# Layer 0's dense products: plain float32 matmuls on unsplit operands in the place of three float32r matmuls on split ones

## The chip, the cores and the metric

The kernel runs on one core of a Trainium2 chip. The metric is device time in microseconds, the median of several executions; lower is better. The engines are TensorE (PE in the profile; PEld is its weight load), VectorE (DVE), ScalarE (ACT), GpSimd (POOL) and SyncE (SP), which issues the DMAs.

## The reference, cut to what matters

A trunk of two layers over 512 tokens of 1024 channels. Only layer 0's mixers and their output projection matter here:

```python
z = rmsnorm(h, mix_norm[j]) @ mix_w_in[j]
y_a = rwkv7_bidir(z[..., :RWKV_COLS], ...)      # 8 heads x 64, one scan per direction
y_b = hyena_bidir(z[..., RWKV_COLS:], ...)      # 512 channels, long filters through an FFT
h = h + jnp.concatenate([y_a, y_b], axis=-1) @ mix_w_out[j]
...
h = h + conv_ffn(h, ...)
h = h + per_layer_embedding(h, p[i], ...)       # sigmoid(rmsnorm(h) @ w_gate) * (p_i @ w_proj)
```

Layer 1 has neighbourhood attention in the mixers' place, then the same two blocks.

## The kernel before

Channels lie on the partitions, 128 at a time, and the 512 tokens along the free dimension. Everything is float32 in DRAM.

**Split products.** A large product is made of three float32r matmuls: each operand is split into a high part, rounded to float32r, and a low part, the rest (`split`, lines 361 to 368; `mm3`, 370 to 373). ScalarE writes the high part, VectorE or GpSimd the low one. The feed-forward blocks, layer 1 and the late output projection (`gemm`, `load_split`) do this too, with their own loops and buffers.

**Layer 0's mixers** (`both_mixers`, from line 703) are one stage with two kinds of work:

- a *main line* of dense products, unit after unit in a fixed order: the input projection (26 tiles of 128 columns, eight products each; `columns`, 859), the projections of the per-layer embeddings (`embedding`, 1384), Hyena's transforms (`forward`, 1403) as products with tables of cosines and sines, the early part of the output projection (`out_early`, 1476: row tiles 0 to 2), and the transform back (`inverse`, 1448);
- *chains* of small steps beside it: the norm (`norm0`, 827), the preparation of each head pair and direction (`rwkv_prep`), the inverses of triangular matrices (`inverse_ab`), the scans over chunks of 64 tokens (`scan`), the group norm and gate (`rwkv_out`), the filters and the products of spectra (`filter_parts`, `spectrum`).

`drive` (670) writes the two out in one order. It keeps a plan (`Pace`, 205 to 313) of when each engine will have done what is written so far; when a chain's next stage is planned to be ready, the stage is written, else the next product of the main line. Where the planned TensorE work of the last 3.4 us falls under 5000 columns, the main line goes first. `in_order` (558) then holds every engine to that written order, so a step that is late on the chip holds up what is written behind it on its engine. The plan's price of a matmul is columns x passes / 2400 us, with 1 pass for float32r, 2 for a transpose and 4 for float32 (lines 272 to 277); that of a VectorE instruction is 0.07 + 0.00106 us a column (282).

**Operands of the main line.** Weights and tables come as slabs of 128x512 float32 (`stream`, 588): up to three are loaded ahead, and up to three more are split ahead (`feed`, 619, when the plan says that the load has landed; `parts`, 581: ScalarE copies to float32r at line 584, GpSimd subtracts). A slab of weights serves four products. The tables of the transforms are stored already split in DRAM and are only cast, the high part by ScalarE (611), the low one by GpSimd (612). The layer's input, the signals, the filters' sums and the spectra are split where they are made. There are 59 slabs.

**After the mixers** `outproj0` (1551) adds the late row tiles of the output projection with `gemm`; its operands come from `out_parts` (1352), which waits until the input projection no longer reads the buffers that they go to.

Of the kernel before, what the change touches and what calls it, by code (L numbers as in the profile page):

```python
# [32 lines left out]
# ---------------------------------------------------------------- layout of the weights  # L33
# [14 lines left out]
# row tiles of layer 0's output projection: those of its early part, and the others  # L48
# [20 lines left out]
def _kc(n):  # L69
    """Row tiles of weights in a chunk of n column tiles."""  # L70
    return (8, 4, 2, 2)[n - 1]
# [13 lines left out]
# columns of the packed per-channel parameters: name -> number of columns  # L85
# [32 lines left out]
# ---------------------------------------------------------------- constants of the shapes  # L118
# [14 lines left out]


def _hi(a):
    a = np.ascontiguousarray(a, dtype=np.float32)
    b = a.view(np.uint32)
    r = ((b >> 12) & 1) + np.uint32(0x7FF)
    return ((b + r) & np.uint32(0xFFFFF000)).view(np.float32)


def _constants():
# [18 lines left out]
    # transforms at the frequencies (2f+1)pi/1024, f < 256; even and odd times apart, which gives those of 511 - f  # L161
# [6 lines left out]
    inv = parts.transpose(0, 2, 1).reshape(4, 2, P, S)  # part, fc, f, time  # L168
    c["dft_i"] = np.ascontiguousarray(inv.transpose(1, 2, 0, 3)).reshape(2, P, 2048)
    # filter features and decay window  # L170
# [10 lines left out]
def _rpb_table(rpb):  # L181
    """Relative position bias as each (16-column query block, head) reads it, both by columns of the grid;
    -1e30 outside the window."""
# [16 lines left out]
    t = np.stack(out, axis=2).reshape(8, 2, P, 3, 256)  # pair, head, q, table, key  # L200
# [3 lines left out]
# ---------------------------------------------------------------- the kernel  # L204
class Pace:
    """Estimates of when what is written so far will have run. The order in which the rest is written follows them;
    nothing that is computed depends on them."""
# [15 lines left out]
    @staticmethod  # L223
    def area(x):
        """Name, first and last row, first and last column."""
        size = math.prod(x.tensor.shape[1:])
        p, f = divmod(x.offset, size)
        p1, f1 = p, f
        for i, (step, n) in enumerate(x.ap):
            if i == 0 and step == size:  # L230
                p1 += n - 1
            elif step < 0:
                f += step * (n - 1)
            else:
                f1 += step * (n - 1)
        return x.tensor.name, (p, p1, f, f1)
# [23 lines left out]
    # TensorE runs at half its clock after a stretch of this many us in which it streamed less than so many columns  # L260
# [5 lines left out]
    def density(self, t):  # L266
        """Columns streamed in the last TICK us before t."""
# [48 lines left out]
class Kern:  # L316
# [5 lines left out]
    # -- helpers  # L322
# [38 lines left out]
    def split(self, h, l, src, scale=None):  # L361
        """h + l = src (* scale), each in float32r."""
# [12 lines left out]
    def load_split(self, src, width, dt=F32):  # L375
        """One chunk of weights: from DRAM and into its two parts."""
# [7 lines left out]
    def gemm(self, wname, g, k0, k1, xs, evac, then=None):  # L384
        """then: what goes in between after two chunks of weights."""
# [77 lines left out]
    def conv3(self, out, u, w, b):  # L463
        """Centred depthwise convolution of width 3 over the tokens."""
# [9 lines left out]
    # -- the whole  # L474
# [42 lines left out]
    def mixer0(self):  # L517
# [5 lines left out]
        # tiles in DRAM  # L523
# [34 lines left out]
    def in_order(self, start):  # L558
        """Keeps the compute engines to the order in which everything from instruction start on is written."""
# [11 lines left out]
    # -- small helpers: slabs of SBUF, a bank of PSUM  # L571
# [9 lines left out]
    def parts(self, src):  # L581
        """A slab's two parts; the second one by GpSimd."""
        h, l = self.slab(F32R), self.slab(F32R)
        self.nc.scalar.copy(h, src)  # L584
        self.tt(l, src, h.bitcast(F32), ALU.subtract, self.nc.gpsimd)
        return h, l

    def stream(self, items):
        """Slabs from DRAM in their two parts, loaded and split ahead of their use. An item with two sources has its
        parts in them."""  # L590
        self.loads, self.split_ = deque(), deque()
        todo = iter(items)

        def load():
            srcs = next(todo, None)
            if srcs is not None:
                t = [self.slab() for _ in srcs]
                for x, y in zip(t, srcs):
                    self.nc.sync.dma_start(out=x, in_=y)
                self.loads.append(t)  # L600

        for _ in range(self.LOADS):
            load()
        yield
        while True:
            t = self.loads.popleft()
            if len(t) == 1:
                r = self.parts(t[0])
            else:
                r = [self.slab(F32R) for _ in t]  # L610
                self.nc.scalar.copy(r[0], t[0])
                self.nc.gpsimd.tensor_copy(out=r[1], in_=t[1])
            self.split_.append(r)
            load()
            yield
# [12 lines left out]
    def weights(self, name, g):  # L628
        """The slabs of a group of columns."""
# [5 lines left out]
        for k in range(0, K // P, KC):  # L635
            nk = min(KC, K // P - k)
            src = self.a[name][base + k * P * W:base + (k + nk) * P * W].rearrange("(p a) -> p a", p=P)
            out += [(src[:, i:i + 512],) for i in range(0, nk * W, 512)]
        return out

    def table(self, name, fc, j):
        src = self.a[name][fc]
        return src[:, j * 1024:j * 1024 + 512], src[:, j * 1024 + 512:j * 1024 + 1024]
# [8 lines left out]
    def put(self, out, in_):  # L652
        """A store, written once its data should be there, so that its queue doesn't wait."""
# [16 lines left out]
    def drive(self):  # L670
        """Stages of the chains as they can go, and the main line between them."""
        nc, pace, over, row = self.nc, self.pace, False, 0
        while self.chains or not over:
            now = pace.now()
            self.flush(now)
            self.feed(now)
# [26 lines left out]
    def both_mixers(self):  # L703
# [26 lines left out]
        def embed():  # L730
            if emb:
                l, g, j = emb.pop(0)
                what = [(a["pT"][l, k],) for k in range(2)] if (g, j) == (0, 0) else []
# [43 lines left out]
        # loads in the order of their use  # L777
# [3 lines left out]
        self.ws = self.stream(items)  # L781
        for k in range(KT):
            nc.sync.dma_start(out=xin[k], in_=a["xT"][k])
            if k == 0:
                next(self.ws)
# [6 lines left out]
        n = PAR_OFF["na_norm"]  # L792
        nc.sync.dma_start(out=self.prm[:, n:], in_=a["params"][:, n:])
# [8 lines left out]
        # 1 - mu; k_a / 2 and 1 - k_a / 2; w0 / 2, a0 / 2  # L802
# [56 lines left out]
    def columns(self, out):  # L859
        """A tile of columns of the input projection."""  # L860
        ps = self.bank()
        for half in range(2):
            hi, lo = self.item()
            for kk in range(4):
                k = half * 4 + kk
                c = slice(kk * P, (kk + 1) * P)
                while len(self.xs) <= k:
                    yield 0
                self.mm3(ps, hi[:, c], lo[:, c], *self.xs[k], k == 0, k == KT - 1)
                if k < KT - 1:  # L870
                    yield 0.65
# [5 lines left out]
        yield 0.65  # L877
# [45 lines left out]
    def rsqrt8(self, sq, scale, eps, op1=ALU.add):  # L923
        """The powers -1/2 of the sums over 64 channels, with the tokens on the partitions."""
# [10 lines left out]
    def spread(self, r):  # L935
        """... over 128 columns a tile of tokens ..."""
# [5 lines left out]
    def back(self, ex):  # L942
        """... and back with the channels on the partitions."""
# [7 lines left out]
    def rwkv_prep(self, m, d, zz):  # L951
        """Of one direction, in the order of its scan and chunk by chunk: k and r with the running decay, the update
# [894 lines left out]
```

## Time and profile before

| | us |
|---|---|
| time, median of 3 runs | 1636.56 |
| lowest and highest of them | 1633.0, 1638.45 |
| the profiled execution, its span | 1633.0 |
| TensorE busy in the span | 1541.6 (94%) |
| VectorE busy in the span | 1047.9 (64%) |
| ScalarE busy in the span | 681.0 (42%) |
| GpSimd busy in the span | 341.3 (21%) |

The span of the profiled execution and the lowest of the times are the same number: nothing of the time that is measured lies around the span.

The profile lists instructions by line, engine, operation and tiles: `b<-xh,w` is a matmul into a PSUM bank `b` from the input's high part `xh` and a slab `w`; `g` are the banks of the later blocks. Nearly every matmul has line 350, that of a helper, and all slabs are called `w`, so groups are told apart by tiles and shapes. "x464" counts instructions; behind the bar stand busy time and the mean ns of one, then the idle time of the engine ahead of them and what ended it. Matmuls overlap, so the mean is from start to end of one, not the distance to the next. The profile names both kinds of matmul f32 and shows float32r on what is written by the other engines alone (fp32r).

### The profile page before, as it was taken

The numbers are of one execution on the slowest core, as the hardware profiler recorded it, in microseconds if no ns is written. First come the engines' busy times: TensorE is split into PE (matmuls) and PEld (weight loads), VectorE is DVE, ScalarE is ACT, GpSimd is POOL, SyncE is SP. The second block draws the span as 40 slices with busy tenths as digits, with TensorE's granted clock in tenths as the row PEclk, the third lists the DMA queues.
The fourth block names the chain that finished last, engine by engine and source line by source line (L and its number), as shares of the span: only waits on it lengthen the run. The fifth ranks groups of instructions, "written<-read, shape, count | busy, mean of one in ns | idle before, by whom it ended". The sixth has DMA issues, their size and how long they took to land.

```text
span 1633.0 us, 24094 instructions
## 1 busy us (share of the span) xinstructions
PE 1541.6 (94%) x9296; PEld 1216.2 (74%) x9296; DVE 1047.9 (64%) x1740; ACT 681.0 (42%) x1082; POOL 341.3 (21%) x286
## 2 busy tenths in 40 slices
PE   7998798979898999999999989999999999999997
PEld 4675576766667888888888778777777888888886
DVE  7579868876876677534684664565666665276654
ACT  6464224333514544313443553565554442144432
POOL 3585525533721200000001322011030000000020
PEclk9999899899999999999999999999999999999999
DMA  6455638465764232222322433323112332322341
GB/s 202 136 141 137 188 105 237 136 215 157 232 214 167 100 103 90 96 99 90 103 91 96 137 116 103 106 83 123 66 65 78 103 104 90 98 88 93 110 142 65
DMA packets 116308, 200.13 MB, mean 123 GB/s; under 512 B 27729, under 2 KB 57297, under 8 KB 116194
## 3 DMA queue, kind: packets, MB, share of 16 engines
q1 hardware_dynamic: 116194, 198.59, 37.9%
q8 instruction: 73, 1.20, 0.3%
q14 instruction: 41, 0.34, 0.1%
HBM read 166.04 MB, written 30.93 MB: 121 GB/s over the span
## 4 chain that ended last, share of the span: by engine, by line
PE 76%; DVE 11%; issue 5%; ACT 3%; DMA 2%; POOL 2%; SPq 2%; POOLq 0%; DVEq 0%; ACTq 0%
PE g L350 60%; PE b L350 11%; DVE w L356 4%; DVE w L353 3%; PE m L350 1%; PE s L350 1%; PE m L1792 1%; ACT w L359 1%; POOL w L356 1%; DVE w L1168 1%; POOL rr L356 0%; ACT oh L364 0%; DVE ol L356 0%; DMA ch_d<-w 0%; POOL nacc L356 0%
## 5 line engine op out<-in xcount | busy, mean ns | idle before, releaser
L356 DVE TENSOR_TENSOR wlo<-wraw,whi 128x1024 fp32r<-128x1024 f32 x186 | 235.6, 1268 | 334.7 <-ACT whi L364 334.5
L364 ACT CAST whi<-wraw 128x1024 fp32r<-128x1024 f32 x186 | 194.2, 1044 | 426.8 <-PE g L350 410.2
L350 PE MATMUL g<-xh,whi 128*128 128x512 f32 x872 | 341.5, 392 | 5.4 <-ACT whi L364 5.4
L350 PE MATMUL g<-xl,whi 128*128 128x512 f32 x872 | 340.5, 390 | 0.0
L350 PE MATMUL g<-xh,wlo 128*128 128x512 f32 x872 | 340.3, 390 | 0.0
L356 POOL TENSOR_TENSOR w<-w 128x512 fp32r<-128x512 f32 (+2 forms) x142 | 184.0, 1317 | 166.7 <-ACT w L584 95.8
L350 PEld LDWEIGHTS g<-xh,whi 128*128 128x128 f32 x872 | 164.2, 188 | 41.2 <-ACT whi L364 5.6
L350 PEld LDWEIGHTS g<-xh,wlo 128*128 128x128 f32 x872 | 164.1, 188 | 34.9 <-DVE wlo L356 0.8
L350 PEld LDWEIGHTS g<-xl,whi 128*128 128x128 f32 x872 | 164.3, 188 | 33.7
L350 PE MATMUL b<-xh,w 128*128 128x512 f32 x464 | 172.4, 427 | 7.4 <-ACT xh L359 7.3
L356 POOL TENSOR_TENSOR nacc<-nsq 128x512 f32<-128x512 f32 x5 | 9.3, 1865 | 779.8 <-ACT nsq L359 779.8
L350 PE MATMUL b<-w 64*64 64x64 f32 (+6 forms) x1884 | 131.2, 271 | 17.5 <-DVE w L353 7.5
L350 PE MATMUL g<-hh,wlo 128*128 128x512 f32 x352 | 139.0, 395 | 0.0
L350 PE MATMUL g<-hl,whi 128*128 128x512 f32 x352 | 139.0, 395 | 0.0
L350 PE MATMUL g<-hh,whi 128*128 128x512 f32 x352 | 138.9, 395 | 0.0
L353 DVE SCALAR_TENSOR_TENSOR c<-u,prm,c 128x511 f32<-128x511 f32 x176 | 126.6, 748 | 6.9 <-ACT c L359 6.3
L350 PEld LDWEIGHTS b<-w 64*64 64x64 f32 (+4 forms) x1884 | 94.6, 142 | 44.1 <-POOL w L356 10.4
L350 PEld LDWEIGHTS b<-xh,w 128*128 128x128 f32 x464 | 91.6, 197 | 36.8 <-ACT xh L359 8.0
L359 ACT ACTIVATE c<-u,prm 128x512 f32<-128x512 f32 x88 | 70.0, 817 | 71.4 <-DVE u L356 71.4
L350 PE MATMUL b<-xl,w 128*128 128x512 f32 x232 | 95.7, 413 | 1.6 <-DVE xl L353 1.4
L356 DVE TENSOR_TENSOR w<-w 128x512 f32<-128x512 f32 (+16 forms) x127 | 88.8, 708 | 3.8 <-DMA w<-hw_d 1.0
L356 DVE TENSOR_TENSOR u<-g,rstd 128x512 f32<-128x512 f32 x104 | 71.5, 687 | 14.2 <-PE g L350 13.4
(178 smaller groups left out, 2344.0 us busy)
## 6 DMA issues: line engine op xcount, KB each, us to landing
wraw<-in_up SPq DMA_DIRECT2D x88, 512.0 KB, 3.5
wraw<-in_down SPq DMA_DIRECT2D x44, 512.0 KB, 3.4
w<-in_mix_w_in SPq DMA_DIRECT2D x52, 256.0 KB, 3.8
wraw<-in_na_w_qkv SPq DMA_DIRECT2D x24, 512.0 KB, 3.5
x<-ch_d SPq DMA_DIRECT2D x16, 640.0 KB, 5.9
ch_d<-w SPq DMA_DIRECT2D x64, 128.0 KB, 2.7
wraw<-in_gate SPq DMA_DIRECT2D x16, 512.0 KB, 3.5
tab<-in_rpb SPq DMA_DIRECT2D x8, 768.0 KB, 4.3
```

What stands on the lines that cost most here:

```text
L350: return self.nc.tensor.matmul(out, lhsT, rhs, start=start, stop=stop)
L353: return self.nc.vector.scalar_tensor_tensor(out=out, in0=in0, scalar=scalar, in1=in1, op0=op0, op1=op1)
L356: return (eng or self.nc.vector).tensor_tensor(out=out, in0=in0, in1=in1, op=op)
L359: return self.nc.scalar.activation(out=out, in_=in_, func=func, **kw)
L364: self.nc.scalar.copy(h, src)
L1168: nc.vector.tensor_reduce(out=x[:, i, 0:i], in_=tv, axis=AX.X, op=ALU.add)
L1792: nc.tensor.transpose(pst[:, i], sc[:, i // 2, (i % 2) * P:(i % 2 + 1) * P], ident)
```

## The change

In the main line of layer 0's mixers, `mm3` on split operands becomes `mm` on the float32 operands themselves. What splits them goes: `parts`, the casts of tables, the split of the layer's input, of the signals, of the spectra and filters and of the first three row tiles of the mixers' output, which stay in their slabs. The tables in DRAM are not split any more and half as large. Weights are loaded six slabs ahead. The late output projection and all that follows keep split operands. Comments and docstrings are dropped, and the numbers that the units yield are true values only.

```diff
-    parts = np.stack([_hi(C), C - _hi(C), _hi(Sn), Sn - _hi(Sn)])
-    fwd = parts.reshape(4, 4, P, 2, P)  # part, tile of times, time, fc, f
-    c["dft_f"] = np.ascontiguousarray(fwd.transpose(3, 2, 0, 1, 4)).reshape(2, P, 2048)
+    parts = np.stack([C, Sn])
+    fwd = parts.reshape(2, 4, P, 2, P)
+    c["dft_f"] = np.ascontiguousarray(fwd.transpose(3, 2, 0, 1, 4)).reshape(2, P, 1024)
...
-    def parts(self, src):
-        h, l = self.slab(F32R), self.slab(F32R)
-        self.nc.scalar.copy(h, src)
-        self.tt(l, src, h.bitcast(F32), ALU.subtract, self.nc.gpsimd)
-        return h, l
...
+    def load(self, n=1):
+        for _ in range(n):
+            src = next(self.todo, None)
+            if src is not None:
+                t = self.slab()
+                self.nc.sync.dma_start(out=t, in_=src)
                 self.loads.append(t)
...
-    LOADS, AHEAD = 3, 3
-
-    def feed(self, now):
-        while self.loads and len(self.split_) < self.AHEAD and self.pace.ready(self.loads[0]) <= now + self.SLACK:
-            next(self.ws)
+    LOADS = 6
 
     def item(self):
-        if not self.split_:
-            next(self.ws)
-        return self.split_.popleft()
+        t = self.loads.popleft()
+        self.load()
+        return t
...
-            x = (self.px.tile([P, S], F32R, name=f"xh{k}"), self.px.tile([P, S], F32R, name=f"xl{k}"))
-            self.split(*x, xin[k], scale=self.par("mix_norm", k))
+            x = self.px.tile([P, S], F32, name=f"xh{k}")
+            self.act(x, xin[k], scale=self.par("mix_norm", k))
...
-                self.mm3(ps, hi[:, c], lo[:, c], *self.xs[k], k == 0, k == KT - 1)
+                self.mm(ps, w[:, kk * P:(kk + 1) * P], self.xs[k], k == 0, k == KT - 1)
...
     def out_parts(self, k, y):
+        if k < EARLY:
+            self.ys[k] = y
+            return
         yield "projected",
...
-            self.mm3(ps, w[0][:, c], w[1][:, c], *self.emb[l][k], k == 0, k == 1)
+            self.mm(ps, self.emb["w"][k][:, c], self.emb[l][k], k == 0, k == 1)
...
-                self.mm3(p, th[:, c], tl[:, c], src[i][0], src[i][1], t == 0, t == 1)
+                self.mm(p, table[:, i * P:(i + 1) * P], src[i], t == 0, t == 1)
...
-            sT.append((self.slab(F32R), self.slab(F32R)))
-            self.split(*sT[t], ps)
+            sT.append(self.slab())
+            nc.scalar.copy(sT[t], ps)
...
-                        self.mm3(acc[q][:, par], yh[:, c], yl[:, c], th[:, tc], tl[:, tc],
-                                 fc == 0 and j == 0 and par == 0, fc == 1 and j == 1 and par == 1)
+                        self.mm(acc[q][:, par], y[:, c], table[:, tc],
+                                fc == 0 and j == 0 and par == 0, fc == 1 and j == 1 and par == 1)
...
-                self.mm3(ps, w[k][0][:, c], w[k][1][:, c], *self.ys[k], k == 0, k == n - 1)
+                self.mm(ps, w[k][:, c], self.ys[k], k == 0, k == n - 1)
...
-            eo.append(self.parts(s))
+            eo.append(s)
...
-            yy[fc, j, j] = self.parts(t[0])
-            yy[fc, j, 1 - j] = self.parts(t[1])
+            yy[fc, j, j], yy[fc, j, 1 - j] = t
```

More of the change, by code (lines that the diff above doesn't have):

```diff
@@ L132 @@
 RO, NRCONST = _offs(RCONST)
[L135 to L139, printed above, removed]
 def _constants():
@@ L164, in _constants @@
     C, Sn = np.cos(ang).astype(f), np.sin(ang).astype(f)
-    parts = np.stack([_hi(C), C - _hi(C), _hi(Sn), Sn - _hi(Sn)])
-    fwd = parts.reshape(4, 4, P, 2, P)
-    c["dft_f"] = np.ascontiguousarray(fwd.transpose(3, 2, 0, 1, 4)).reshape(2, P, 2048)
-    inv = parts.transpose(0, 2, 1).reshape(4, 2, P, S)
-    c["dft_i"] = np.ascontiguousarray(inv.transpose(1, 2, 0, 3)).reshape(2, P, 2048)
+    parts = np.stack([C, Sn])
+    fwd = parts.reshape(2, 4, P, 2, P)
+    c["dft_f"] = np.ascontiguousarray(fwd.transpose(3, 2, 0, 1, 4)).reshape(2, P, 1024)
+    inv = parts.transpose(0, 2, 1).reshape(2, 2, P, S)
+    c["dft_i"] = np.ascontiguousarray(inv.transpose(1, 2, 0, 3)).reshape(2, P, 1024)
     tl = np.linspace(0.0, 1.0, S, dtype=f)[:, None]
@@ L579, in bank @@
         return self.pb.tile([P, 512], F32, name="b")[:, 0:n]
-    def parts(self, src):
-        h, l = self.slab(F32R), self.slab(F32R)
-        self.nc.scalar.copy(h, src)
-        self.tt(l, src, h.bitcast(F32), ALU.subtract, self.nc.gpsimd)
-        return h, l
-    def stream(self, items):
[L591 to L599, printed above, removed]
-                self.loads.append(t)
[L602 to L615, printed above, removed]
-    LOADS, AHEAD = 3, 3
-    def feed(self, now):
-        while self.loads and len(self.split_) < self.AHEAD and self.pace.ready(self.loads[0]) <= now + self.SLACK:
-            next(self.ws)
+    def stream(self, items):
+        self.loads = deque()
+        self.todo = iter(items)
+    def load(self, n=1):
[4 more added lines that the diff above has]
+                self.nc.sync.dma_start(out=t, in_=src)
+                self.loads.append(t)
+    LOADS = 6
     def item(self):
-        if not self.split_:
-            next(self.ws)
-        return self.split_.popleft()
+        t = self.loads.popleft()
+        self.load()
+        return t
     def weights(self, name, g):
@@ L637, in weights @@
             src = self.a[name][base + k * P * W:base + (k + nk) * P * W].rearrange("(p a) -> p a", p=P)
-            out += [(src[:, i:i + 512],) for i in range(0, nk * W, 512)]
+            out += [src[:, i:i + 512] for i in range(0, nk * W, 512)]
         return out
     def table(self, name, fc, j):
-        src = self.a[name][fc]
-        return src[:, j * 1024:j * 1024 + 512], src[:, j * 1024 + 512:j * 1024 + 1024]
+        return self.a[name][fc][:, j * 512:j * 512 + 512]
     def start(self, prio, gen, *wait):
@@ L675, in drive @@
             self.flush(now)
-            self.feed(now)
             lag = max(pace.now(nc.vector), pace.now(nc.scalar)) > now + self.LAG
@@ L732, in embed @@
                 l, g, j = emb.pop(0)
-                what = [(a["pT"][l, k],) for k in range(2)] if (g, j) == (0, 0) else []
+                what = [a["pT"][l, k] for k in range(2)] if (g, j) == (0, 0) else []
                 unit(self.embedding(l, g, j), *what, *(self.weights(f"proj{l}", g) if j == 0 else []))
@@ L780, in both_mixers @@
         fw4 = [self.slab() for _ in range(2)]
-        self.ws = self.stream(items)
+        self.stream(items)
         for k in range(KT):
@@ L784, in both_mixers @@
             if k == 0:
-                next(self.ws)
+                self.load(3)
             if k == 0:
@@ L792, in both_mixers @@
         n = PAR_OFF["na_norm"]
+        self.load(self.LOADS - 3)
         nc.sync.dma_start(out=self.prm[:, n:], in_=a["params"][:, n:])
@@ L862, in columns @@
         for half in range(2):
-            hi, lo = self.item()
+            w = self.item()
             for kk in range(4):
                 k = half * 4 + kk
-                c = slice(kk * P, (kk + 1) * P)
                 while len(self.xs) <= k:
                     yield 0
-                self.mm3(ps, hi[:, c], lo[:, c], *self.xs[k], k == 0, k == KT - 1)
+                self.mm(ps, w[:, kk * P:(kk + 1) * P], self.xs[k], k == 0, k == KT - 1)
                 if k < KT - 1:
-                    yield 0.65
+                    yield 0.86
         if self.normed:
@@ L876, in columns @@
             self.late.append((out, ps))
-        yield 0.65
+        yield 0.86
     def low_rank(self):
@@ L1398, in embedding @@
         self.put(self.pj_d[l * 8 + g * 4 + j], t)
-        yield 1.3
+        yield 1.7
     def forward(self, src, j, out):
         nc = self.nc
-        th, tl = self.item()
+        table = self.item()
         while len(src) < 4:
@@ L1412, in forward @@
                 i = par * 2 + t
-                c = slice(i * P, (i + 1) * P)
-                self.mm3(p, th[:, c], tl[:, c], src[i][0], src[i][1], t == 0, t == 1)
+                self.mm(p, table[:, i * P:(i + 1) * P], src[i], t == 0, t == 1)
                 if i < 3:
-                    yield 0.65
+                    yield 0.86
             ps.append(p)
@@ L1426, in forward @@
         out += [f0, f1]
-        yield 0.65
+        yield 0.86
     def load_signals(self, ss):
@@ L1463, in inverse @@
                     tabs[fc, j] = self.item()
-                th, tl = tabs[fc, j]
+                table = tabs[fc, j]
                 for par in range(2):
-                    yh, yl = yy[fc, j, par]
+                    y = yy[fc, j, par]
                     tc = slice(par * 256, par * 256 + 256)
@@ L1469, in inverse @@
                         c = slice((m0 + q) * P, (m0 + q + 1) * P)
[L1470 to L1472 removed]
+                        self.mm(acc[q][:, par], y[:, c], table[:, tc],
+                                fc == 0 and j == 0 and par == 0, fc == 1 and j == 1 and par == 1)
+                    yield 0.86
         for q in range(2):
@@ L1478, in out_early @@
         n = WEIGHTS["mix_w_out_a"][0] // P
-        while None in self.ys[:n] or self.pace.ready(self.ys[n - 1]) > self.pace.now() + self.SLACK:
+        while None in self.ys[:n] or self.pace.ready(self.ys[:n]) > self.pace.now() + self.SLACK:
             yield 0
@@ L1488, in out_early @@
             for k in range(n):
-                self.mm3(ps, w[k][0][:, c], w[k][1][:, c], *self.ys[k], k == 0, k == n - 1)
+                self.mm(ps, w[k][:, c], self.ys[k], k == 0, k == n - 1)
                 if k < n - 1:
-                    yield 0.65
+                    yield 0.86
             self.tt(xin[j], ps, xin[j], ALU.add)
             self.put(self.h_d[g * 4 + j], xin[j])
-            yield 0.65
+            yield 0.86
     def hyena_out(self, m, acc, x0, s):
```

2 lines of the change are left out of this document (removed).

## The prediction, made before the changed kernel was run

> **What bounds the kernel now.** I read the stretches of the span first, since layer 0's mixers and the rest have different limits. Columns: length of the stretch, busy time of each engine with its instructions, granted TensorE clock, share of the DMA engines, GB/s.
>
> ```profile
> 0.00:120.00 120.00, 105.60 (x562) 74.41 (x562) 80.72 (x125) 65.88 (x112) 69.75 (x78) 0.97 0.52 159
> 120.00:300.00 180.00, 152.46 (x1732) 113.92 (x1729) 150.86 (x308) 64.58 (x126) 89.55 (x83) 0.91 0.57 159
> 300.00:440.00 140.00, 126.96 (x1388) 96.40 (x1388) 108.48 (x207) 54.40 (x113) 65.25 (x55) 0.95 0.59 185
> 440.00:484.00 44.00, 36.91 (x377) 25.68 (x376) 35.64 (x66) 9.80 (x25) 20.95 (x16) 0.96 0.67 227
> 484.00:504.00 20.00, 14.62 (x113) 13.38 (x113) 12.54 (x21) 8.90 (x15) 1.64 (x1) 0.95 0.46 160
> sum 504.00, PE 436.56 PEld 323.79 DVE 388.23 ACT 203.55 POOL 247.13; mean PE 87.31 PEld 64.76 DVE 77.65 ACT 40.71 POOL 49.43
> ```
>
> The change touches the first 504 us alone: at 503.99 the late output projection starts, on the same split operands as before. Its 1129 us up to the end I take as unchanged. In the 504 us TensorE is busy for 436.56 and idle for 67.4; VectorE is busy for 388.23, and in 120 to 300 for 150.86 of 180. So TensorE leads, with VectorE close behind in one stretch. What ended TensorE's idle time:
>
> ```profile
> PE b L350 <- DVE uv L356: 11.1, 15, 3.0
> PE b L350 <- DVE w L356: 9.4, 7, 2.6
> PE b L350 <- DVE w L353: 7.5, 3, 5.0
> PE b L350 <- ACT xh L359: 7.3, 2, 6.5
> PE b L350 <- DVE uv L1296: 6.0, 5, 2.7
> PE b L350 <- DVE r L1281: 5.5, 5, 1.9
> ```
>
> Columns: total, times, longest. 39.5 us of it are waits for VectorE (11.1 + 9.4 + 7.5 + 6.0 + 5.5), by small steps of the chains. The dense products hardly wait for their split operands, but for the first: 6.5 us, the stage's filling.
>
> Does the main line or a chain set the end of the stage? The timeline of TensorE at the end of the last scan:
>
> ```profile
> 483.46 0.45 PE L350 MATMUL b<-x,uv 128*64 128x64 f32 x8
> 483.84 1.67 PE L350 MATMUL b<-w 128*128 128x256 f32 x12
> ...
> 489.28 3.78 PE L350 MATMUL b<-w 128*128 128x256 f32 x30
> 492.91 0.60 PE L946 MATMUL b<-con,w 128*128 128x128 f32 x4
> ...
> 493.80 4.81 PE L350 MATMUL b<-w 128*128 128x256 f32 x36
> 503.99 0.80 PE L350 MATMUL g<-xh,whi 128*128 128x512 f32 x1 [5.38 <-ACT whi L364]
> ```
>
> The last scan step is at 483.46, and all 96 instructions (12 + 30 + 36 and 18 more) of the inverse transform, which are main line, still come after it; then 5.38 us of draining. The main line is never out of work while a scan runs. So the stage ends when TensorE has got through main line plus chains, and a longer dense product lengthens it unless idle time goes.
>
> **The change part by part.** *Products, TensorE.* The groups of the stage:
>
> ```profile
> L350 PE MATMUL b<-xh,w 128*128 128x512 f32 x464 | 172.4, 427 | 7.4 <-ACT xh L359 7.3 <-POOL w L356 0.2
> L350 PE MATMUL b<-xl,w 128*128 128x512 f32 x232 | 95.7, 413 | 1.6 <-DVE xl L353 1.4
> L350 PE MATMUL b<-w 128*128 128x512 f32 x192 | 51.5, 414 | 1.7 <-DVE w L356 1.7
> L350 PE MATMUL b<-w,con 128*128 128x512 f32 x24 | 14.0, 667 | 0.9 <-DVE w L356 0.9
> L350 PE MATMUL b<-w 128*128 128x256 f32 x96 | 13.0, 291 | 0.0
> ```
>
> The first, second, third and fifth are the products to be changed, three instructions each: (464 + 232 + 192) / 3 = 296 of 512 columns and 96 / 3 = 32 of 256. The fourth is plain float32 at the same shape: 12 calls, 24 records, so one plain product is two instructions, and the 984 become 656. Means of overlapping instructions are latencies; what counts is the distance between starts:
>
> ```profile
> 301.03 0.62 PE L350 MATMUL b<-xh,w 128*128 128x512 f32 x2
> ...
> 305.21 0.62 PE L350 MATMUL b<-xh,w 128*128 128x512 f32 x2
> ```
> ```profile
> 79.62 1.02 PE L350 MATMUL b<-w,con 128*128 128x512 f32 x2
> 80.47 0.60 PE L1043 MATMUL b<-con,w 128*128 128x128 f32 x4
> ```
> ```profile
> 309.10 1.02 PE L350 MATMUL b<-sg,gup 128*128 128x512 f32 x2
> 310.05 0.45 PE L350 MATMUL b<-uv,x 128*64 128x64 f32 x8
> ```
>
> Six split products go by between 301.03 and 305.21: 0.697 us each. A plain one takes 0.85 where a full-array instruction follows and 0.95 where another shape does. A long run of them is not in the trace; 0.85 and 0.95 are the two ends. I take 0.86, near the first, since most products follow their like. 296 x (0.86 - 0.697) = 48 us (45 to 75). For 256 columns: (492.91 - 489.28) / 30 x 3 = 0.363 split; plain there isn't shown, from half of 0.85 to half of 0.95; at 0.43, 32 x 0.067 = 2 us (2 to 4). Sum: **+50 us of TensorE time** (47 to 79).
>
> The Trainium skill, page "FP8 and Floating Point Precision", section "TensorE Precision Notes", gives true FP32 four passes of the array; at a third of 0.697 a pass that would be an estimated 0.93 and +69 us for the 296. The row with 0.85 speaks against that last step, and the row decides.
>
> *Splits, ScalarE and GpSimd.*
>
> ```profile
> L584 ACT CAST w<-w 128x512 fp32r<-128x512 f32 x86 | 51.2, 616 | 20.5 <-DMA w<-in_mix_w_in 10.7 <-DVE w L356 5.0 <-DMA w<-in_mix_w_out_a 1.9
> L611 ACT CAST w<-w 128x512 fp32r<-128x512 f32 x12 | 7.2, 620 | 0.1
> L356 POOL TENSOR_TENSOR w<-w 128x512 fp32r<-128x512 f32 x86 | 124.5, 1459 | 137.6 <-ACT w L584 95.8 <-issue 11.7 <-DVE w L356 10.2
> L612 POOL CAST w<-w 128x512 fp32r<-128x512 f32 x12 | 9.8, 818 | 6.7 <-PE b L350 2.6 <-issue 2.3 <-DMA w<-in_dft_i 1.7
> ```
>
> All four go: 58 us of ScalarE and 134 of GpSimd's 247. VectorE loses the second parts of the layer's input, the signals and the early outputs, 15 instructions. None of it is on TensorE's path now, so it is worth nothing by itself: its cover is the main line, split three items ahead. With it goes one more wait: the casts sit in ScalarE's queue and waited 10.7 us for weights, with the chains' activations behind them.
>
> *VectorE beside GpSimd.* This is what the removal is worth. First the mixers' groups, then the same kinds of operation in layer 0's feed-forward stretch, 508 to 950 us:
>
> ```profile
> L356 DVE TENSOR_TENSOR w<-w 128x512 f32<-128x512 f32 x51 | 48.7, 972 | 2.1 <-DMA w<-hw_d 1.0 <-ACT w L1314 0.4
> L353 DVE SCALAR_TENSOR_TENSOR w<-w,prm 128x512 f32<-128x512 f32 x38 | 40.6, 1078 | 2.7 <-POOL w L356 2.5
> L353 DVE SCALAR_TENSOR_TENSOR w<-w,prm 128x511 f32<-128x511 f32 x24 | 23.7, 988 | 2.0 <-ACT w L359 1.4
> ```
> ```profile
> L353 DVE SCALAR_TENSOR_TENSOR c<-u,prm,c 128x511 f32<-128x511 f32 x88 | 63.3, 749 | 3.4 <-ACT c L359 3.2
> L356 DVE TENSOR_TENSOR c<-ga,c 128x512 f32<-128x512 f32 x22 | 15.1, 688 | 0.0
> ```
> ```profile
> 124.90 1.03 DVE L356 TENSOR_TENSOR w<-w 128x9 f32<-128x9 f32 x1
> 128.84 0.22 DVE L356 TENSOR_TENSOR w<-w 128x36 f32<-128x36 f32 x1
> ```
>
> 51 x (972 - 688) + 38 x (1078 - 749) + 24 x (988 - 749) = 33 us of lengthening in three groups; a 9-column operation took 1.03 us while GpSimd ran, a 36-column one 0.22 when it didn't. The Trainium skill, page "SBUF — State Buffer", section "Who interferes with whom", says that a VectorE instruction with two SBUF inputs and a GpSimd instruction that reads SBUF lock each other out for a whole instruction; the two rows just above agree.
>
> How much of TensorE's waiting ends with it isn't shown. Ends: nothing, and all 39.5 us of waits for VectorE. I take the share of GpSimd's work that goes, 134 / 247 = 0.54 of it: **-21 us**.
>
> *Clock.* The mean granted clock of the 504 us is 0.94 (the stretches above, weighted), so 30 us of clock weren't granted, in stretches of small steps and idling. Fuller stretches should get some back; ends 0 and 30, I take a quarter, since the small steps themselves stay: **-7 us**.
>
> *Other edits, nothing.* The loads: six items ahead on SP's queue instead of three raw and three split, one item being four products or 3.4 us, so 20 us of lead; if it weren't enough, TensorE itself would now wait for the weights, by some 2 us a time. The tables come in 8 loads where 16 were. The three early outputs are read in place, without a split and without waiting for the projection's end. At the start the first eight products still go at the pace of ScalarE's scaling and squares. The tail after the last product (5.4 us) stays.
>
> Sum: 50 - 21 - 7 = +22 us. The profiled execution's span is 1633.0 us, which becomes 1655; the median of the three runs, 1636.56, is 3.6 above it, and I predict against that: **1658.6 us**.
>
> **The rivals.** *Full price.* The order is written out from planned times: 0.853 us for a plain product and 0.64 for a split one, against 0.86 and 0.697 by the rows. Until now the main line ran 9% slower than planned, which gave VectorE room (it is planned at 0.61 us where 688 ns is its best); that room falls to 1%. If that undoes the port's relief, idle time stays: 1636.6 + 50 = 1687, or some us more. For it: the plan knows nothing of the port. Against it: the lengthening is large, 33 us of 388 in three groups alone.
>
> *VectorE was the bound (faster).* In 120 to 300 it was busy for 84% of the time and TensorE idle for 27.5 us. If its queue, stretched by the lock-out of the page on SBUF, sets the pace of the chains up to 484, then its relief ends nearly all 40 us of waits and gives back 20 of the clock's 30: 50 - 60 = -10, 1627 us. It decides from 50 us of savings on, out of the 70 that there are. Against it: the main line still has work when the last scan ends, and outside 120 to 300 VectorE is busy for 73% only.
>
> *A draw.* Savings of 45 to 55 us: within 5 us of 1636.6.
>
> **How the numbers follow.** A measurement of this kernel can tell about 0.3%, 4.9 us, from no change. Forecast, 1642 to 1677 (savings of 10 to 45 us): 0.49. Full price, above 1677: 0.19. Draw, 1632 to 1641: 0.15. VectorE the bound, below 1632: 0.17. Faster 0.17, same 0.15, slower 0.68. The range 1629 to 1690 leaves out the deeper half of the fast case and the part of full price in which the plain product costs well over 0.86: some 0.2 together. The likeliest case's own range is 1642 to 1677.
>
> **What would show it.** Right: 656 instructions for these products, 0.86 us between plain products in a run; GpSimd's busy time in the mixers near 113 us (247 - 134); the 128x512 groups of VectorE with two SBUF sources near 830 ns (972 less half of the excess); TensorE's idle time in the stage down to some 46 us (67.4 - 21), and the late projection starting near 526 us, all later stretches as long as now. Wrong: a run of plain products at 0.95 or more; waits for VectorE as long as before; weights' DMAs among TensorE's waits; a start of the late projection before 504, which would say that VectorE was the bound; or any change after that start.

## The result, and the profile after

| | before | after |
|---|---|---|
| median, us | 1635.64 (4 runs) | 1673.42 (4 runs) |
| lowest and highest | 1633.0, 1638.45 | 1672.08, 1674.92 |
| span of the profiled execution | 1633.0 | 1673.1 |
| start of the late output projection | 503.99 | 542.28 |
| from there to the end | 1129.0 | 1130.8 |

The ratio after to before is 1.0225, 95% interval 1.0207 to 1.0242. The changed kernel is slower by 38 us, where 22 were forecast. 1673.4 us lies inside the forecast's range of 1629 to 1690, which is wide: the likeliest case's own range ended at 1677. The profiled execution of the changed kernel took 1674.92 us for a span of 1673.1, so 1.8 us of the measured time lie around the span; that span and lowest time of the kernel before are the same number is no sign that nothing lies around its span, and the section on its profile was wrong to conclude so.

Line numbers are 7 to 36 lower after the change (350 became 343, 356 became 349, 353 became 346, 946 became 910). The view by stretches for both kernels, columns as in the prediction: first the mixers' stage, then the rest; before, then after.

```profile
0.00:504.00 504.00, 436.56 (x4161) 323.79 (x4161) 388.23 (x726) 203.55 (x388) 247.13 (x230) 0.94 0.57 173
504.00:1633.00 1129.00, 1105.09 (x5136) 892.45 (x5136) 659.69 (x1015) 477.44 (x694) 94.15 (x56) 0.99 0.30 100
```
```profile
0.00:542.00 542.00, 483.68 (x3832) 260.61 (x3832) 323.38 (x710) 150.25 (x287) 112.07 (x132) 0.95 0.51 154
542.00:1673.00 1131.00, 1106.55 (x5136) 893.43 (x5136) 659.49 (x1016) 477.44 (x695) 94.14 (x56) 0.99 0.31 100
```

Read the two lines of the stage as time minus busy time: TensorE is busy for 47.1 us more (483.68 - 436.56), and idle for 58.3 us where it was 67.4, so 9.1 less. 47.1 - 9.1 is the 38 us. TensorE has 329 instructions fewer (4161 - 3832), as 656 products' instructions in the place of 984 would have it. GpSimd's busy time fell by 135 us, VectorE's by 65, ScalarE's by 53, and nearly none of that reached the end of the stage. The rest of the kernel, in the second line of each, is as it was.

VectorE's groups with two sources in SBUF, and the waits of TensorE, both of the changed kernel up to 542 us (the waits: total, times, longest):

```profile
L349 DVE TENSOR_TENSOR w<-w 128x512 f32<-128x512 f32 x51 | 34.8, 707 | 5.4 <-DMA w<-hw_d 4.2
L346 DVE SCALAR_TENSOR_TENSOR w<-w,prm 128x512 f32<-128x512 f32 x38 | 29.2, 785 | 6.1 <-ACT w L352 5.9
L346 DVE SCALAR_TENSOR_TENSOR w<-w,prm 128x511 f32<-128x511 f32 x24 | 20.4, 850 | 2.8 <-ACT w L352 2.1
```
```profile
PE b L343 <- DVE uv L349: 12.3, 10, 5.7
PE b L343 <- DVE w L346: 9.3, 4, 5.1
PE b L343 <- DMA x<-ch_d: 7.8, 4, 3.2
PE b L343 <- ACT xh L352: 5.9, 1, 5.9
PE b L910 <- ACT w L902: 5.1, 2, 3.0
PE b L343 <- DVE w L349: 4.3, 4, 1.9
PE b L1017 <- DVE w L349: 3.2, 1, 3.2
PE b L343 <- DMA uv<-vt_d: 1.5, 2, 0.9
PE b L1007 <- DVE w L349: 1.3, 1, 1.3
```

VectorE's groups were relieved of 28 of the 33 us of lengthening that the prediction counted: 972 ns fell to 707, further than the 830 that it gave as a sign, 1078 to 785, 988 to 850. That agrees with the lock-out that the Trainium skill's page "SBUF — State Buffer", section "Who interferes with whom", describes. But TensorE's waits for VectorE fell only from 44 us (the 39.5 of the prediction and 4.9 in three smaller rows) to 31 (12.3 + 9.3 + 4.3 + 3.2 + 1.3 and 0.9 in two smaller rows). Waits for transfers, mostly of the scans' operands, rose from 2.7 to 9.6; those for GpSimd went from 3.7 to none, and those for ScalarE stayed, 15 before and 16 after, though with another part, its spreading of the norms (5.1).

The end of the stage, from the timeline of TensorE after the change:

```profile
486.18 0.45 PE L343 MATMUL b<-x,uv 128*64 128x64 f32 x8
486.57 3.70 PE L343 MATMUL b<-w 128*128 128x512 f32 x8
490.10 1.02 PE L343 MATMUL b<-w,con 128*128 128x512 f32 x2
...
499.21 1.02 PE L343 MATMUL b<-sg,gup 128*128 128x512 f32 x2
500.07 38.01 PE L343 MATMUL b<-w 128*128 128x512 f32 x120
542.28 0.50 PE L343 MATMUL g<-xh,whi 128*128 128x512 f32 x1 [4.19 <-ACT whi L357]
```

The last scan step is at 486.18; before it was at 483.46. The chains are as long as they were, though their engines have less to do. What stands behind the last scan step grew from 20.5 to 56 us, with 38 us of products alone at its end. In both kernels the last step of the chains on TensorE is the product with the gate, `b<-sg,gup`, at 499.21 after and, before, here:

```profile
493.34 1.02 PE L350 MATMUL b<-sg,gup 128*128 128x512 f32 x2
```

Before, only the 4.81 us of products at 493.80 stood behind it.

### The profile page after: what moved, and what is told of

Its sections match the earlier page's. It is cut to its first block, busy times and chain, and to the rows that moved or that the text cites. A ratio compares the mean times of both kernels' runs of the same rounds, so it can differ in the third digit from the quotient of the medians.

```text
span 1673.1 us, 23101 instructions
## 1 busy us (share of the span) xinstructions
PE 1590.2 (95%) x8968; PEld 1154.0 (69%) x8968; DVE 982.9 (59%) x1725; ACT 627.7 (38%) x981; POOL 206.2 (12%) x188
## 4 chain that ended last, share of the span: by engine, by line
PE 83%; DVE 7%; DMA 3%; SPq 2%; ACT 2%; issue 1%; POOL 1%; POOLq 0%; DVEq 0%; ACTq 0%
PE g L343 59%; PE b L343 19%; DVE w L349 3%; DVE w L346 2%; PE s L343 1%; PE m L343 1%; DMA x<-ch_d 1%; PE m L1756 1%; SPq L1142 0%; POOL rr L349 0%; DVE w L1132 0%; ACT oh L357 0%; DVE ol L349 0%; POOL nacc L349 0%; PE m L1707 0%
## 5 line engine op out<-in xcount | busy, mean ns | idle before, releaser
L343 PE MATMUL b<-xh,w 128*128 128x512 f32 x416 | 213.2, 642 | 6.0 <-ACT xh L352 5.9
L343 PE MATMUL b<-w 32*32 32x32 f32 (+6 forms) x1836 | 164.9, 294 | 14.1 <-DVE w L346 9.3
L343 PEld LDWEIGHTS b<-xh,w 128*128 128x128 f32 x416 | 75.3, 199 | 81.8 <-issue 67.6
L349 POOL TENSOR_TENSOR w<-w 128x256 f32<-128x256 f32 (+1 forms) x56 | 60.5, 1101 | 146.7 <-DVE w L349 59.1
L343 PE MATMUL g<-wlo,xh 128*128 128x512 f32 x192 | 77.6, 404 | 0.0
L343 PEld LDWEIGHTS g<-hh,whi 128*128 128x128 f32 x352 | 65.9, 187 | 16.4
```

The source lines that it names most:

```text
L343: return self.nc.tensor.matmul(out, lhsT, rhs, start=start, stop=stop)
L349: return (eng or self.nc.vector).tensor_tensor(out=out, in0=in0, in1=in1, op=op)
```

## The experiments

Two theories at first. **P**: the products' TensorE time decides, and the removal of the splits is worth the little that the trace shows. **V**: VectorE's relief is worth the 28 us that I forecast, and the products cost more than 50. Four runs separate products, splits and chains. After them a third theory was needed, and eight more runs test it: that the *written order* makes the idle time. Below, the stage's end is the start of the late projection, and idle time is that end less TensorE's busy time, both from the view by stretches. The last scan step is the last `b<-x,uv` in the timeline of TensorE. Ratios are to runs of the kernel before on the same chip, whose medians were 1635.5 to 1636.5.

| run | time, us | ratio to before, interval | last scan step | stage up to | idle in it |
|---|---|---|---|---|---|
| before | 1635.6 |  | 483 | 504 | 67 |
| after | 1673.4 | 1.0207 to 1.0242 | 486 | 542 | 58 |
| split products without second parts | 1618.8 | 0.9872 to 0.9929 | 453 | 489 | 58 |
| plain products beside unread splits | 1670.6 | 1.0182 to 1.0244 | 492 | 541 | 57 |
| half of the projection left out | 1632.3 | 0.9960 to 0.9996 | 487 | 502 | 99 |
| before, second parts by VectorE | 1667.0 | 1.0164 to 1.0231 | 511 | 537 | 97 |
| after, 3 passes planned | 1647.1 | 1.0042 to 1.0091 | 483 | 517 | 42 |
| after, VectorE's measured price | 1653.3 | 1.0064 to 1.0131 | 499 | 524 | 48 |
| after, both | 1649.2 | 1.0058 to 1.0106 | 500 | 516 | 42 |
| after, 2.5 passes planned | 1631.6 | 0.9964 to 0.9989 | 479 | 499 | 35 |
| 3 passes planned, with unread splits | 1664.2 | 1.0145 to 1.0194 | 516 | 535 | 55 |
| before, both of the plan's prices as measured | 1673.2 | 1.0195 to 1.0260 | 527 | 542 | 92 |
| before, VectorE's measured price | 1675.7 | 1.0222 to 1.0277 | 519 | 543 | 99 |
| before, 0.8 passes planned | 1659.1 | 1.0122 to 1.0179 | 513 | 529 | 80 |

The column of the last scan step sorts the runs. In the three slower plans of the kernel before, the chains end 30 to 44 us later than before and the stage ends 15 to 24 us behind them; in the changed kernel as it came, the chains end on time and 56 us follow.

**Splits without their second parts, products still split.**

```diff
     def parts(self, src):
-        h, l = self.slab(F32R), self.slab(F32R)
+        h = self.slab(F32R)
         self.nc.scalar.copy(h, src)
-        self.tt(l, src, h.bitcast(F32), ALU.subtract, self.nc.gpsimd)
-        return h, l
+        return h, h
```

The same for the tables, the layer's input and the signals. ScalarE's casts stay.

> The kernel before, with three float32r matmuls a product, but no second parts in the main line: the high part stands in the low part's place, so GpSimd's 134 us of subtractions and casts and VectorE's part of the splits are gone, and the outputs differ. It tells what the removal of the splits is worth by itself. Theory P (the price of the products decides; the trace after shows idle time down by 8 us and the chains' instructions by 5): 1636 - 13 = 1623 us. Theory V (VectorE's relief is worth what I forecast, 28 us, and the products cost more than 50): 1608. Theory N (the splits were wholly hidden): 1636.

Measured 1618.8 us, 17 less than before: between P and V. The last scan step of this run:

```profile
453.40 0.45 PE L350 MATMUL b<-x,uv 128*64 128x64 f32 x8
```

That is 30 us earlier than before, so here, with VectorE relieved as much as by the change (324.6 us busy in the stage), the chains do end sooner.

**Plain products, with the splits put back as work that nobody reads.**

```diff
+    def ahead(self):
+        t, table = self.loads.popleft()
+        if table:
+            h, l = self.slab(F32R), self.slab(F32R)
+            self.nc.scalar.copy(h, t)
+            self.nc.gpsimd.tensor_copy(out=l, in_=t)
+        else:
+            self.parts(t)
+        self.split_.append(t)
+        self.load()
```

> The changed kernel with the splits put back as work that nobody reads: the same casts by ScalarE, subtractions by GpSimd and VectorE, three slabs loaded and three split ahead; the products stay plain. It tells what the products' price is by itself. P: 1673 + 13 = 1686 us. V: 1673 + 28 = 1701. N: 1673. Under each theory VectorE's 128x512 groups with two SBUF sources are back near 970 ns.

Measured 1670.6, not slower than without the splits. The lengthening is back all the same, in the groups of VectorE up to 541 us:

```profile
L349 DVE TENSOR_TENSOR w<-w 128x512 f32<-128x512 f32 x51 | 49.1, 980 | 2.7 <-POOL w L349 2.1
L346 DVE SCALAR_TENSOR_TENSOR w<-w,prm 128x512 f32<-128x512 f32 x38 | 35.3, 948 | 5.0 <-ACT w L352 2.4 <-POOL w L349 2.2
```

980 ns against 707, and no time lost by it. So N holds in this pair, and 17 us in the other: neither P nor V explains both. Against the kernel before, this run has the splits and differs in the products (and in the order): they cost 35 us here.

**Half of the input projection left out.**

```diff
-                self.mm(ps, w[:, kk * P:(kk + 1) * P], self.xs[k], k == 0, k == KT - 1)
+                if kk % 2 == 0:
+                    self.mm(ps, w[:, kk * P:(kk + 1) * P], self.xs[k], k == 0, k == KT - 2)
```

> The changed kernel with every second product of the input projection left out: 104 of 208, 104 x 0.858 = 89 us of TensorE's time, so the outputs differ. If TensorE's time is the bound all along (P): 1673 - 89 = 1584 us. If the chains have a length of their own, about 486 us up to the last scan step in both traces, the main line's 56 us behind the last scan go and the rest turns into idle time: 1673 - 56 = 1617.

Measured 1632.3: 41 us less, not 89. The stage:

```profile
0.00:502.00 502.00, 402.64 (x3625) 228.90 (x3626) 329.47 (x711) 150.08 (x287) 112.82 (x132) 0.88 0.55 167
```

TensorE's busy time fell by 81 us (483.68 - 402.64), its idle time rose by 41 (99.4 - 58.3), and the granted clock fell to 0.88. The last scan step stayed at 487. So P is wrong as I put it: with less to do on the main line, the chains set the end. The 1617 of that theory was too low by what follows the last scan step:

```profile
486.81 0.45 PE L343 MATMUL b<-x,uv 128*64 128x64 f32 x8
487.19 3.72 PE L343 MATMUL b<-w 128*128 128x256 f32 x16
493.33 0.99 PE L343 MATMUL b<-con,w 128*128 128x2 f32 x8
497.14 0.66 PE L911 MATMUL b<-con,w 128*128 128x128 f32 x4 [2.81 <-ACT w L903]
497.63 1.50 PE L343 MATMUL b<-sg,gup 128*128 128x512 f32 x2
501.81 0.80 PE L343 MATMUL g<-xh,whi 128*128 128x512 f32 x1 [2.68 <-ACT whi L357]
```

The last heads still need their group norm and gate, small steps for which TensorE waits, and with these 15 us 1617 becomes the 1632 measured. (Lines between are left out.) But 487 is the chains' length under this order only: without second parts, above, they ended at 453.

**The kernel before, second parts by VectorE.**

```diff
-        self.tt(l, src, h.bitcast(F32), ALU.subtract, self.nc.gpsimd)
+        self.tt(l, src, h.bitcast(F32), ALU.subtract)
```

> The kernel before with the second parts of slabs subtracted by VectorE, not GpSimd: 98 x 0.69 = 68 us more work for VectorE, and the lengthening by GpSimd's subtractions, 50 to 65 us, gone. P: VectorE's total hardly moves and TensorE bounds, 1636 within 8 us. V: a shorter queue for GpSimd's own chain steps and an unlocked port make it 1636 - 15 = 1621 or faster.

Measured 1667.0, slower by 31 us: both expectations fell. (86 of the 98 moved; the tables' 12 casts stayed with GpSimd.) VectorE's groups up to 530 us and the stage:

```profile
L356 DVE TENSOR_TENSOR w<-w 128x512 fp32r<-128x512 f32 x86 | 65.1, 773 | 22.7 <-ACT w L584 22.0
L356 DVE TENSOR_TENSOR w<-w 128x512 f32<-128x512 f32 x49 | 34.7, 727 | 5.8 <-DMA w<-hw_d 5.3
```
```profile
0.00:537.00 537.00, 440.48 (x4160) 328.76 (x4160) 397.99 (x811) 207.10 (x390) 125.44 (x144) 0.91 0.54 162
```

The lengthening of VectorE's instructions is gone (727 ns), VectorE's total is only 10 us higher, yet TensorE is idle for 96.5 us. The subtractions now stand in VectorE's queue among the chains' steps and waited 22 us there for ScalarE's casts; how much of the 31 us comes from that isn't shown.

**Third theory: room.** The idea: engines keep the order that is written from planned times. If a plain product is planned at its true 0.853 us, the main line takes just as long as planned, and a VectorE that is slower than its plan (0.688 us, planned at 0.613) is waited for. A split product was planned at 0.64 and took 0.697, so it left VectorE time. This is the mechanism of the prediction's rival *full price*. Two edits of the plan alone:

```diff
-            passes = 1 if ins.ins[0].dtype == F32R else 2 if ins.is_transpose else 4
+            passes = 1 if ins.ins[0].dtype == F32R else 2 if ins.is_transpose else 3 if n >= 256 and ins.tile_size[0] == 128 else 4
```
```diff
-        return 0.07 + n * 0.00106
+        return 0.145 + n * 0.00106
```

> The changed kernel with plain products planned at 3 passes (0.64 us, what a split product was planned at) while they take 0.858: only the written order changes. Theory room (the rival full price: a main line slower than its plan gives VectorE time): idle time falls from 53 to below 35 us, 1655 us or less. Theory PE (TensorE's own time is the bound in any order): within 8 us of 1673. Theory chains (the chains' length decides): the chains are written later against the main line, the last scan step moves behind 486, and the time rises to 1680 or more.

> The changed kernel with VectorE planned at its measured price, 0.145 + 0.00106 us a column (0.688 at 512) in the place of 0.07 + 0.00106 (0.613): order alone. If TensorE's waits for VectorE come from too short a plan, they fall by a third or more (from 31 us) and the time goes to 1660; if not, within 8 us of 1673.

Measured 1647.1 and 1653.3. The same instructions in another order are 26 and 20 us faster. With VectorE's price, TensorE's waits for it fell from 31 us to 24, a quarter where a third was expected; the time fell further than the 1660 expected. The stage with 3 passes planned, then its longest waits up to 510 us:

```profile
0.00:517.00 517.00, 475.38 (x3832) 259.91 (x3832) 326.11 (x710) 148.34 (x285) 111.17 (x132) 0.96 0.53 162
```
```profile
PE b L343 <- DVE uv L349: 10.2, 15, 3.4
PE b L343 <- DVE w L349: 7.8, 5, 2.7
PE b L343 <- ACT xh L352: 6.0, 1, 6.0
PE b L1408 <- DMA w<-s_d: 4.8, 4, 3.0
```

Idle time is 41.6 us where it was 58.3. Theory *room* asked for less than 35 by the count that leaves the first wait of 6 us out (53 for the changed kernel); by that count it is 36: nearly, and the time is below the 1655 asked for. Theory *chains* is out: the last scan step moved to 483, not behind 486.

The pair of it, with the unread splits at the same short plan:

> The plain products with the unread splits, at the short plan of 3 passes: the pair of the run with the short plan alone, under a second order. If the splits' removal is really worth nothing beside plain products, the two are within 8 us of each other, as 1673.4 and 1670.6 were. If that was an accident of the order, this one is 13 us or more slower than its pair.

Measured 1664.2 against 1647.1: 17 us. So the removal of the splits went with 17 us beside plain products at the short plan, as that of the second parts did beside split ones. At the change's own order it was worth nothing; by the expectation, that belongs to this order and not to plain products as such. But each of these pairs differs in its order too, since the plan sees the splits. With the splits kept, plain products cost 28 us at the short plan (1664.2 against 1636.5), where they cost 35 at the change's own prices.

The kernel before with both of its prices corrected, then with one, and with more room:

```diff
-            passes = 1 if ins.ins[0].dtype == F32R else 2 if ins.is_transpose else 4
+            passes = 1.09 if ins.ins[0].dtype == F32R else 2 if ins.is_transpose else 4
```

(The second run has VectorE's price alone, as above; the third 0.8 in this line alone.)

> The kernel before with the same correction of VectorE's price and split products planned at 1.09 passes (0.697 us a product, as measured): order alone. If a too short plan costs the idle time, 1620 us or less and a kernel faster than both; if the room that the main line gave is lost with it, 1640 to 1655.

> The kernel before with VectorE's measured price alone, products planned at 1 pass as they were. If the loss with both corrections (1673) came from the room that went with the products' true price, this one is 1636 or faster, 1620 if it gains what the changed kernel gained; if it came from VectorE's price, 1655 or more.

> The kernel before with split products planned at 0.8 pass each, 0.51 us against 0.697 measured: more room. If room is what a plan lacks here too, idle time falls from 61 to about 45 us and the time to 1622; if this order is near its best already, 1636 within 8 us or slower.

Measured 1673.2, 1675.7 and 1659.1: each slower than its 1636, by 37, 40 and 23 us. VectorE's price, which gained 20 us for the changed kernel, costs the kernel before 40, and more room costs it 23. Theory *room* fails there: the order before is better than each of the three others that were tried.

More room for the changed kernel, and both corrections:

> The changed kernel with plain products planned at 2.5 passes, 0.53 us. If more room is always better, idle time goes under 30 us and the time under 1645; if the gain of the short plan was spent at 3 passes, 1647 within 8 us; if chains written too late against the main line cost more than the waits, 1660 or more.

> The changed kernel with both corrections that helped: 3 passes and VectorE at its measured price. If they act on the same waits, 1647 within 8 us; if on different ones, 1630 to 1638, level with the kernel before.

Measured 1631.6 with 2.5 passes and 1649.2 with both. The two corrections act on the same time, not one on top of the other. More room helped again: 1631.6 is under the 1645 expected, and idle time is 35 us, 29 by the count without the first wait, where under 30 was expected. The stage with 2.5 passes planned, and its longest waits:

```profile
0.00:499.00 499.00, 464.07 (x3833) 255.91 (x3834) 323.69 (x711) 148.51 (x285) 109.57 (x132) 0.98 0.56 168
```
```profile
PE b L343 <- DVE uv L349: 6.8, 13, 2.6
PE b L343 <- ACT xh L352: 6.3, 2, 6.0
PE g L343 <- ACT whi L357: 5.9, 1, 5.9
PE b L343 <- DVE uv L1260: 5.3, 7, 1.4
PE b L343 <- DVE r L1245: 3.3, 3, 2.9
```

Against the change's own order TensorE is idle for 23 us less (34.9, was 58.3) and busy for 20 us less with the same instructions (464.07, was 483.68), at a granted clock of 0.98 where it was 0.95. This is the fastest version found that computes the whole layer: ratio to the kernel before is 0.9976, interval 0.9964 to 0.9989, 4 us. Its stage ends 19 us behind the last scan step, close to the 15 that the group norm and gate took with half of the projection left out, so here the chains nearly set the end.

## Why the prediction was right, and where it wasn't

- **The products, +50 us**: right. The run of products alone at 500.07 has 56 instructions of 512 columns and the 64 of the inverse transform (the line shows the first one's shape); at 0.429 and 0.2155 us they make 24.0 + 13.8 = 37.8 of its 38.01. So a plain product is 0.858 us in a run, as taken, and one of 256 columns 0.431: 47.7 + 2.2 = 50 us. The Trainium skill's page "FP8 and Floating Point Precision", section "TensorE Precision Notes", gives true FP32 four passes, which would be an estimated 0.2145 us each; the trace shows two instructions a product, not the passes. A split product's three instructions take 0.232 each, so the prediction's estimate from them, 0.93, was too high. TensorE's busy time rose by 47 us; the 3 us less are about what the clock gave back (its term is below).
- **The splits themselves worth nothing, all of the gain through VectorE's relief**: the relief came, 28 of the 33 us (972 to 707 ns), with GpSimd at 112 us where 113 were forecast. That the gain of 9 us came through it isn't shown: with the lengthening back (980 ns), the time was the same, 1670.6.
- **The waits, -21 us, and the clock, -7**: too much, and these are the terms that were mis-sized; 12 and 4 us of the 16 that the forecast was short. Idle time fell by 9 us, and the clock's missing part went from 0.06 x 504 = 30 us to 0.05 x 542 = 27. I took the share of GpSimd's work that goes as the share of the waits that go; nothing in the trace said so, and the sum left out that new waits can take the place of old ones. Waits for VectorE fell by 13 us and for GpSimd by 4, but those for transfers rose by 7 and for ScalarE by 1. The runs with and without splits say 17 us for the removal in two of three pairs, and nothing in the order that the change came with.
- **"The stage ends when TensorE has got through main line plus chains"**: true of the changed kernel, where 38 us of products follow the last gate; before, only by some 5 us. The chains' last scan step is near 485 in both, and with half of the projection gone the chains alone set the end, 15 us behind theirs. The prediction counted only TensorE's time, and not that the chains' end moves with the order: it lay between 453 and 527 us in the runs.
- **The rivals**: *full price* has the right mechanism for the changed kernel, the order that is written from the plan. 12 of the 50 us came back, where it said none and the forecast 28. *VectorE was the bound* is wrong for this order: VectorE's busy time fell by 65 us and the last scan step came 3 us later, not sooner.

So the number came out inside a wide range, and the step of the sum that gives the products was right, while the savings were 12 us where 28 were forecast.

What stays open: how much of the 38 us belongs to the products and how much to the order. Between the best orders that were run, the whole change costs nothing, -4 us; between the two orders as they came, +38. Without the splits on both sides, plain products cost 13 us at their best order (1631.6 against 1618.8, which has been run under one order only and still has ScalarE's casts). That the kernel before has no better order was tried with three others, which doesn't show it. Those runs, and the first four, all came with orders of their own, since the plan sees less or more work: each difference up to some 20 to 40 us among them, the size of what order alone did, may be the order's in part, the 17 us of the two pairs included.

## What to carry to other kernels

Where an order is written out from planned times, an edit of an operation's price is also an edit of the order, and here the order was worth nearly as much as the products' price: up to 42 us against 50. Before such a change is judged, run it under two or three plans. And an engine that is relieved off the path gives time back only where the order lets its earlier results be used: 65 us of VectorE's time went here, and the chains ended no sooner; in the run without second parts 64 us went, and they ended 30 us sooner.

## What the runs showed of the hardware that wasn't expected

A plain float32 product of 512 columns cost 23% more TensorE time than three float32r ones (0.858 against 0.697 us), where the plan's prices say 33% (0.853 against 0.64): the latter's instructions take 0.232 each, the former's two 0.429. And the granted clock was higher where TensorE idled less: 0.98 with 35 us of idle time in the stage, 0.94 to 0.96 with 42 to 67, 0.88 to 0.91 with 80 to 99. With 2.5 passes planned the same instructions took 20 us less busy time. That the idling itself lowers the clock is not shown by these runs.
